# Encoder layer on one core: a sixth Strassen group in the input projection, and attention whose instructions stand in text order on every engine

## The chip, the cores and the metric

One core of a Trainium2 chip runs the whole layer. The metric is the device time of one execution in microseconds (us). The kernel before takes 1931.56 us, the median of 3 runs (1931.3 to 1931.82).

## The reference, cut to what matters

The input x is 1024 tokens by 1024 features in float32; the tokens form a grid of 16 by 64.

```python
h = x + 0.5 * swiglu(rms_norm(x, ffn1_norm), ...)          # D_FF = 2816
u = rms_norm(h, mix_norm)
z = u @ w_in                                               # 1024 x 4352
qa, ka, va, qb, kb, vb, ga, gb = split(z)
ya = neighbourhood_attention_2d(qa, ka, va, na_rpb)        # 8 heads of 64, bias by offset
yb = windowed_gqa_sink(rope(qb), rope(kb), vb, sink_logit) # 8 heads, 2 for k and v, window 128
merged = sigmoid(ga) * (ya @ w_branch_a) + sigmoid(gb) * (yb @ w_branch_b)
h = h + merged @ w_out
h = h + 0.5 * swiglu(rms_norm(h, ffn2_norm), ...)
return rms_norm(h, final_norm)
```

## The kernel before

**Arithmetic.** Every float32 factor is kept as a high part and a low part (`split`: ScalarE copies the high part, VectorE subtracts to get the low part, L93 and L94). A product is then three matmuls (`mm3`, L145, L147, L149: high times high, high times low, low times high). A matmul works on 128 x 128 weights and 512 columns.

**Stages.** The first FFN's hidden layer (an order written by hand), its down projection together with the norm that yields u, the input projection, attention, the two branch projections, the merge with w_out, the second FFN, the last norm. The FFNs, w_out and most columns of w_in go by Strassen: `products` takes two pairs of 128 columns as a group and makes 7 products of 24 matmuls with 512 columns for it, where plain multiplication takes 4 x 48 matmuls. VectorE makes the sums of blocks, and `store_z` brings the results out.

**The input projection.** w_in has 34 column blocks of 128. Five Strassen groups (`groups`) make 20 of them, the q, k and v blocks and two of the 16 gate blocks (numbers 18 to 33). The 14 gate blocks left (`gates`) are multiplied plainly, and serve as filler in attention.

**Attention.** 64 units go through a pipe three deep: 32 of the windowed GQA (`units_b`), then 32 of the neighbourhood attention (`units_a`). A unit is two heads' scores for 128 queries. Its three steps are

- `scores` (S): 4 matmuls into two banks of tag d (L1294, L1295); VectorE adds the bias and takes the minimum of the negated row (L1299), ScalarE takes exp with the row's sum (L1302), VectorE the reciprocal (L1305) and scales one head (L1306), ScalarE scales the other (L1307);
- `turn` (T): 6 transposes into two more banks of tag d (L1315), and a split of each (L93, L94);
- `values` (V): 6 matmuls into a bank of tag g (L1334, in units_a L1329), a copy on ScalarE (L1247, L1268) and additions on VectorE (`write`, L1249, L1269, L1272).

There are 4 banks of tag d and 4 of tag g. The loop over n issues S of unit n, filler, T of unit n-1, filler, V of unit n-2. The filler is a generator: `gate` yields after each of its 8 steps of 6 matmuls into two banks of tag g. At step 4 the next gate's weights are split (`load_w`, 128 x 1024), and at its end ScalarE copies the two banks out (L1143). `rate` lets 1.66 steps through per unit. After the last gate, `branch_b` (8 blocks of 4 steps) multiplies yb by w_branch_b: it splits a weight block (128 x 512), opens the gate with a sigmoid (L1195, 128 x 1024) and multiplies each bank by it (L1213). `branch_a` then does the like for ya. `units_a` adds bias and mask itself (`load_bias`, L1089).

**Who sets the order.** In the program of before a scheduler orders attention: the text hands it the instructions, and it places them on each engine's queue by its own estimate of what is ready. Only the first stage is ordered by hand. Each engine then takes its queue from the front and waits on semaphores.

## Time and profile before

| what | value |
| --- | --- |
| median of 3 runs | 1931.56 us |
| the profiled execution | 1931.21 us |
| its span, first to last instruction | 1929.4 us |
| mean granted TensorE clock | 0.999 |
| PE (matmul) busy | 1919.3 us, 99% |
| DVE (VectorE) busy | 1434.0 us, 74% |
| ACT (ScalarE) busy | 944.2 us, 49% |
| POOL (GpSimd) busy | 296.1 us, 15% |
| moved by DMA | 298.70 MB, 155 GB/s |

The profiled execution is 1.8 us longer than its span, and stands 0.35 us under the median. On the time axis of the trace, the groups of the input projection stand at about 675 to 843 us, attention at about 844 to 1126 us, the branch projections behind it. The views used below are the page (busy times, the chain that ended last, the groups of instructions), the waits of PE, the timeline of one engine (start, duration, engine, line, operation, output <- inputs, shape, and in brackets the idle time before and what ended it), and tables of busy time by stretch. A matmul's duration in the timeline overlaps the next one's: the distance between two starts says what a matmul costs.

### The profile page before, as it was taken

The page shows a single profiled execution, that of the slowest core. Times are in us where ns is not written, and L with a number is a line of the kernel's source. Part 1 is how long each engine was busy: PE and PEld are TensorE (multiplying, and loading weights), DVE is VectorE, ACT ScalarE, POOL GpSimd, SP SyncE. Part 2 cuts the span into 40 slices and gives each one's busy share as a digit, 9 for nine tenths or more (in the row PEclk, how much of TensorE's full clock was granted, in tenths as well). Part 3 has the DMA queues.
Part 4 walks back from the last instruction along what each step waited for, and adds up shares of the span by engine and source line. Part 5 has one row for each costly group of instructions (what it writes and reads, how often), then busy time and mean ns, then how long its engine had stood idle before and what let it go on. Part 6 is the DMA issues. An engine that isn't in the chain of part 4 may idle for free.

```text
span 1929.4 us, 25478 instructions
## 1 busy us (share of the span) xinstructions
PE 1919.3 (99%) x8956; PEld 1602.7 (83%) x8956; DVE 1434.0 (74%) x2560; ACT 944.2 (49%) x1826; POOL 296.1 (15%) x432
## 2 busy tenths in 40 slices
PE   9999999999999999999999999999999999999998
PEld 8888888888888888888888888888888888888886
DVE  8987765668957778678888856889676566569864
ACT  7532333344446543477777862365333333344453
POOL 0011100013300112211122231010111001005210
PEclk9999999999999999999999999999999999999999
DMA  6244323285334467753459676443422322493341
GB/s 267 95 167 166 138 100 125 87 298 215 92 106 138 158 202 240 218 166 102 116 130 195 188 240 212 170 153 121 147 98 103 127 87 106 145 340 114 115 142 61
DMA packets 151745, 298.70 MB, mean 155 GB/s; under 512 B 14912, under 2 KB 64448, under 8 KB 151616
## 3 DMA queue, kind: packets, MB, share of 16 engines
q1 hardware_dynamic: 123072, 210.53, 33.3%
q0 software_dynamic: 27824, 85.48, 13.3%
q8 instruction: 71, 1.16, 0.2%
q10 hardware_dynamic: 720, 1.05, 0.1%
q14 instruction: 58, 0.48, 0.1%
HBM read 210.50 MB, written 88.27 MB: 155 GB/s over the span
## 4 chain that ended last, share of the span: by engine, by line
PE 96%; DVE 2%; ACT 1%; DMA 0%; issue 0%; POOLq 0%; POOL 0%; DVEq 0%
PE g L145 18%; PE g L147 18%; PE g L149 18%; PE d L149 12%; PE d L145 12%; PE d L147 12%; PE d L1315 2%; PE g L1329 1%; PE d L1294 1%; PE d L1295 1%; PE g L1334 1%; PE d L138 1%; DVE ar L94 0%; DMA ahead<-in_w_in_dram 0%; DMA n1c<-in_ffn_norm_dram 0%
## 5 line engine op out<-in xcount | busy, mean ns | idle before, releaser
L145 PE MATMUL g<-ar,ws 128*128 128x512 f32 x1128 | 422.6, 395 | 0.3 <-DVE fa L602 0.3
L147 PE MATMUL g<-ar,ws 128*128 128x512 f32 x1128 | 416.7, 390 | 0.0
L149 PE MATMUL g<-ar,ws 128*128 128x512 f32 x1128 | 416.3, 390 | 0.0
L145 PE MATMUL d<-ar,ws 128*128 128x512 f32 x736 | 281.9, 390 | 0.5 <-ACT ws L309 0.5
L147 PE MATMUL d<-ar,ws 128*128 128x512 f32 x736 | 281.4, 389 | 0.1
L149 PE MATMUL d<-ar,ws 128*128 128x512 f32 x736 | 281.2, 389 | 0.1
L149 PEld LDWEIGHTS g<-ar,ws 128*128 128x128 f32 x1128 | 211.7, 188 | 44.8
L147 PEld LDWEIGHTS g<-ar,ws 128*128 128x128 f32 x1128 | 211.8, 188 | 44.6
L145 PEld LDWEIGHTS g<-ar,ws 128*128 128x128 f32 x1128 | 206.4, 188 | 36.4 <-issue 0.7
L312 DVE TENSOR_TENSOR ws<-raw,ws 128x512 fp32r<-128x512 f32 x204 | 139.3, 689 | 98.9 <-ACT ws L309 97.9
L309 ACT CAST ws<-raw 128x512 fp32r<-128x512 f32 x204 | 125.0, 620 | 142.2 <-PE g L149 63.8
L145 PEld LDWEIGHTS d<-ar,ws 128*128 128x128 f32 x736 | 138.1, 188 | 29.4 <-ACT ws L309 0.9
L147 PEld LDWEIGHTS d<-ar,ws 128*128 128x128 f32 x736 | 138.1, 188 | 29.3 <-DVE ar L814 0.5
L149 PEld LDWEIGHTS d<-ar,ws 128*128 128x128 f32 x736 | 138.1, 188 | 29.1 <-DVE ws L312 0.5
L93 ACT CAST ws<-raw 128x512 fp32r<-128x512 f32 (+1 forms) x121 | 81.0, 669 | 144.7 <-PE d L149 66.7
L94 DVE TENSOR_TENSOR ws<-raw,ws 128x512 fp32r<-128x512 f32 (+1 forms) x119 | 94.0, 792 | 60.7 <-ACT ws L93 60.5
L415 POOL DMA_DIRECT2D hid<-fx x91 | 49.3, 542 | 432.3 <-DVE fx L475 288.6
L93 ACT CAST ar<-raw 128x512 fp32r<-128x512 f32 (+1 forms) x83 | 56.0, 679 | 93.7 <-PE g L147 55.0
L94 DVE TENSOR_TENSOR ws<-ar,ws 128x512 fp32r<-128x512 f32 x114 | 98.2, 866 | 4.0 <-ACT ws L93 3.9
L145 PE MATMUL g<-ws,ws 128*128 128x512 f32 x232 | 90.9, 392 | 0.0
L149 PE MATMUL g<-ws,ws 128*128 128x512 f32 x232 | 90.4, 390 | 0.0
L147 PE MATMUL g<-ws,ws 128*128 128x512 f32 x232 | 90.3, 389 | 0.0
(313 smaller groups left out, 3604.8 us busy)
## 6 DMA issues: line engine op xcount, KB each, us to landing
raw<-hid SPq DMA_DIRECT2D x70, 512.0 KB
hid<-fx POOLq DMA_DIRECT2D x91, 256.0 KB, 2.3
ar<-in_ffn_w_down_dram SPq DMA_DIRECT2D x32, 512.0 KB
raw<-in_ffn_w_up_dram SPq DMA_DIRECT2D x31, 512.0 KB
raw<-in_ffn_w_gate_dram SPq DMA_DIRECT2D x27, 512.0 KB
raw<-in_w_in_dram SPq DMA_DIRECT2D x27, 512.0 KB
hid<-fa POOLq DMA_DIRECT2D x51, 256.0 KB, 2.6
ar<-zs_d POOLq DMA_DIRECT2D x48, 256.0 KB, 5.0
```

The source lines that it names most:

```text
L93: nc.scalar.copy(dst_hi, src)
L94: (eng or nc.vector).tensor_tensor(dst_lo, src, f32v(dst_hi), op=ALU.subtract)
L138: nc.tensor.transpose(pt[:, c * P:(c + 1) * P], xs[:, (half * 4 + c) * P:(half * 4 + c + 1) * P], ident)
L145: nc.tensor.matmul(b, lhs[0], r[0], start=first, stop=False, **kw)
L147: nc.tensor.matmul(b, lhs[0], r[1], start=False, stop=False, **kw)
L149: nc.tensor.matmul(b, lhs[1], r[0], start=False, stop=last, **kw)
L309: nc.scalar.copy(w[0][:, :512], a)
L312: nc.vector.tensor_tensor(w[0][:, 512:], a, f32v(w[0][:, :512]), op=ALU.subtract)
L415: nc.gpsimd.dma_start(hid[PRODUCTS.index(p), i], src)
L1294: nc.tensor.matmul(b[:, :nw], un["q"][s], un["kd"][s][:, k0 * P:k1 * P], start=True, stop=False)
L1295: nc.tensor.matmul(b[:, :nw], un["q"][s], un["kl"][s][:, k0 * P:k1 * P], start=False, stop=True)
L1315: nc.tensor.transpose(pt[:, i * P:(i + 1) * P], un["pr"][s][:, i * P:(i + 1) * P], ident)
```

## The change

1. **A sixth group.** The gate blocks 20 to 23 join the Strassen groups; 10 gates are left to attention.
2. **Text order.** `attention()` stands in a block that keeps the order of the text on VectorE, ScalarE, TensorE and the two queues that issue DMAs. The scaling of the probabilities (`scaled`) is taken out of `scores` and stands behind `turn`. `write` is cut in two: the copy stays in `values`, the addition follows the next unit's scores.
3. **Filler in halves.** A step of 6 matmuls now yields after 3. Each of the two filling calls of a unit gets 1.6 halves while n < 50, then 2, then 3 from n = 62, so that a gate (16 halves) takes exactly five units, and `branch_b` (64 halves) and the first part of `branch_a` (12) stand inside the attention.
4. **Gates by tanh.** sigmoid(x) becomes (tanh(x/2) + 1) / 2: a tanh on ScalarE, and (t + 1) times the bank in one VectorE instruction (L1293); the half goes into the scale of w_out's down projection (1.0 becomes 0.5). One ACT_TABLE_LOAD is gone from the program (4, now 3).
5. **Bias and mask.** The 16 additions of L1089 move to the first FFN's down projection and go by way of DRAM (`bm_d`); `fetch_bias` reads them back.
6. **Buffers and places.** The last group's results use another ring of slots; two early weight loads of the groups use other tiles and are issued at t = 0 and 1, not 3 and 4; u is fetched early; a unit's sink copies and its two output additions of 64x128 become one each; the splits of y (128 x 1024) move from GpSimd to VectorE.

```diff
+    def mm3_halves(banks, first, last, lhs, rhs):
+
+        parts = [(w, b, r[k], k) for w, k in ((0, 0), (0, 1), (1, 0)) for b, r in zip(banks, rhs)]
+        for i, (w, b, r, k) in enumerate(parts):
+            nc.tensor.matmul(b, lhs[w], r, start=first and w + k == 0, stop=last and w == 1)
+            if i == 2:
+                yield
...
+    bm_d = dram.tile([8, 2, P, 384], F32, name="bm_d")
...
+    def bias_add(h):
+        for e in range(2):
+            o = biased[0][4 + e]
+            pin(nc.vector.tensor_tensor(o.rearrange("p (d r w) -> p d r w", d=3, r=ROWS),
+                                        biased[0][2 + h % 2].rearrange("p (r d w) -> p d r w", d=3, w=8),
+                                        biased[0][e].rearrange("p (d r w) -> p d r w", d=3, r=ROWS), op=ALU.add))
...
-    groups = [[(12, 13), (14, 15)], [(16, 17), (0, 1)], [(4, 5), (8, 9)], [(2, 3), (6, 7)], [(10, 11), (18, 19)]]
+    groups = [[(12, 13), (14, 15)], [(16, 17), (0, 1)], [(4, 5), (8, 9)], [(2, 3), (6, 7)], [(10, 11), (18, 19)],
+              [(20, 21), (22, 23)]]
...
+    def gate_split(late=False):
+        h, l, r = ws4(), ws4(), mix["gate"]
+        split(h, l, r, None, late)
+        mix["gate"] = [a.rearrange("p (c f) -> p c f", f=P) for a in (h, l)]
...
+    held = [main.tile([P, 512], F32, tag="hs", bufs=6, name=nm_("hs")) for _ in range(6)]
+
+    def bias_at(hp, s, e):
+        k = 2 * (hp % 2) + s
+        return held[k][:, :384] if e else fa[:, 384 * k:384 * k + 384]
+
+    def fetch_bias(hp):
+        for s in range(2):
+            for e in range(2):
+                nc.sync.dma_start(bias_at(hp, s, e), bm_d[2 * hp + s, e])
...
         w = mix.pop("gate")
         bs = [bank("g"), bank("g")]
         for k, c in enumerate((4, 5, 6, 7, 0, 1, 2, 3)):
-            mm3(bs, k == 0, k == NC8 - 1, (w[0][:, c, :], w[1][:, c, :]), [u_half(c, n) for n in range(2)])
-            yield
+            yield from mm3_halves(bs, k == 0, k == NC8 - 1, (w[0][:, c, :], w[1][:, c, :]), [u_half(c, n) for n in range(2)])
+            if k < NC8 - 1:
+                yield
             if k in steps:
...
         gt = xs4()
         for n in range(2):
             nc.scalar.copy(gt[:, n * 512:(n + 1) * 512], bs[n])
         nc.gpsimd.dma_start(g_d[dc * P:(dc + 1) * P, :], gt)
+        yield
...
+    def open_gate(dc):
+        r = mix["rb", dc]
+        pin(nc.scalar.activation(r, r, AF.Tanh, scale=0.5))
+
+    def split_w(i):
+        mix["w", i] = branch_w(nc.gpsimd if i >= 10 else None, mix.pop(("wr", i)))
 
     def branch_b():
 
-        for c in range(2, 4):
-            split_y(Y_B[c], c * P, nc.vector if c == 2 else nc.gpsimd)
         for g in (4, 6):
             new_ar(g, F32)
-        nxt = branch_w(wb[0], 0, nc.vector), gate_b(0)
+        split_y(Y_B[2], 2 * P, nc.vector)
         for dc in range(NC8):
-            w, rb = nxt
             bs = [bank("dg"[dc % 2]) for _ in range(2)]
-            yield from branch_mm(bs, w, Y_B)
-            if dc + 1 < NC8:
-                nxt = branch_w(wb[0], dc + 1, nc.vector), gate_b(dc + 1)
+            mm = branch_mm(bs, mix.pop(("w", dc)), Y_B)
+            for c in range(4):
+                drain(mm, 1)
+                yield
+                drain(mm, 1)
+                if c < 3:
+                    yield
+                if c == 0:
+                    if dc == 0:
+                        split_y(Y_B[3], 3 * P, nc.vector)
+                    split_w(dc + 1)
+                    fetch_w(dc + 2)
+                elif c == 1:
+                    open_gate(dc)
+                    if dc + 1 < NC8:
+                        fetch_gate(dc + 1)
+            rb = mix.pop(("rb", dc))
...
             for n in range(2):
                 sl = slice(n * 512, (n + 1) * 512)
-                nc.vector.tensor_tensor(merged(dc)[:, sl], bs[n], rb[:, sl], op=ALU.mult)
+                nc.vector.scalar_tensor_tensor(out=merged(dc)[:, sl], in0=rb[:, sl], scalar=1.0, in1=bs[n],
+                                               op0=ALU.add, op1=ALU.mult)
+            yield
...
     def filler():
         for dc, nxt in zip(gates, gates[1:] + [None]):
             if nxt is not None:
-                yield from gate(dc, {4: lambda: mix.update(gate=load_w(win[0], GA + nxt * P))})
+                yield from gate(dc, {0: lambda: gate_fetch(nxt, raw4()), 5: gate_split})
             else:
-                yield from gate(dc, {0: lambda: [fetch_y(c * P) for c in range(2)],
-                                     4: lambda: [split_y(Y_B[c], c * P, nc.gpsimd) for c in range(2)],
-                                     5: lambda: [fetch_y(c * P) for c in range(2, 4)]})
+                yield from gate(dc, {0: lambda: [fetch_w(0), fetch_w(1)] + [fetch_y(c * P) for c in range(2)],
+                                     2: lambda: fetch_gate(0),
+                                     4: lambda: [split_y(Y_B[0], 0, nc.vector), fetch_y(2 * P)],
+                                     5: lambda: split_w(0),
+                                     6: lambda: [split_y(Y_B[1], P, nc.vector), fetch_y(3 * P)]})
         yield from branch_b()
         for i in range(2):
             branch_a(i)
-            for _ in range(3):
-                drain(a_mm[i][1], 1)
-                yield
+            for c in range(3):
+                for _ in range(2):
+                    drain(a_mm[i][1], 1)
+                    yield
...
                     lo = mix["lo"][:HD, c % 2]
                     nc.scalar.copy(lo, o[HD:])
-                    for s in range(2):
-                        nc.vector.tensor_tensor(ybox["b"][s * HD:s * HD + HD, c, :], o[:HD, s, :], lo[:, s, :], op=ALU.add)
+                    yield
+                    nc.vector.tensor_tensor(ybox["b"][:, c], o[:HD], lo, op=ALU.add)
...
+        un["sums"] = ssum, rc
+
+    def scaled(un):
+
+        ssum, rc = un["sums"]
         nc.vector.reciprocal(rc, ssum)
         nc.vector.tensor_scalar_mul(un["pr"][0], un["pr"][0], rc[:, 0:1])
         nc.scalar.activation(un["pr"][1], un["pr"][1], AF.Copy, scale=rc[:, 1:2])
...
+    n_b = 50
+    spent = 0.0
+
+    def filling(n):
         nonlocal spent
-        spent += rate * share
+        spent += len(gates) * 8 / n_b if n < n_b else 2 if n < 62 else 3
         drain(fill, int(spent))
...
+    def attention():
+
+        nonlocal pipe, prep
+        rest = iter(())
+        for n in range(1 << 30):
+            got = next(source, None)
+            if got is not None:
+                scores(got)
+            drain(rest)
+            pipe.insert(0, got)
+            for hp, n0 in preps.items():
+                if n == n0:
+                    prep = prep_a(hp)
+            if prep:
+                drain(prep, 1)
+            filling(n)
+            if len(pipe) > 1 and pipe[1] is not None:
+                turn(pipe[1])
+            if got is not None:
+                scaled(got)
+            if prep:
+                drain(prep, 1)
+            if n >= 26 and (n - 26) % 8 == 0 and n < 58:
+                fetch_bias((n - 26) // 8)
+            if n in (56, 57, 59):
+                fetch_y(512 + min(n - 56, 2) * P)
+            if n in (59, 60, 62):
+                split_y(Y_A[min(n - 59, 2)], 512 + min(n - 59, 2) * P, nc.vector)
+            filling(n)
+            if len(pipe) > 2 and pipe[2] is not None:
+                rest = values(pipe[2])
+            pipe = pipe[:3]
+            if not any(pipe):
+                break
+        drain(rest)
+        drain(fill)
+
+    by_text[0] = True
+    with tc.manual_schedule(engines={E.DVE, E.Activation, E.PE, E.SP, E.Pool}):
+        attention()
+    by_text[0] = False
...
-    down = Down(4, wo[0], 1.0, place, quarter, {k: left_d[i] for i, k in enumerate(("P5", "P6", "P3", "P7"))},
+    down = Down(4, wo[0], 0.5, place, quarter, {k: left_d[i] for i, k in enumerate(("P5", "P6", "P3", "P7"))},
```

Three places show what moved. First PE, at the change from one gate to the next among the units of GQA. The banks g_7085 and g_7086 belong to the gate that ends, g_7346 and g_7347 to the next; L162 is the filler's matmul, L1440 V, L1397 and L1398 S, L1421 T. In before, L145 to L149 are the filler, g_7514 and g_7515 the gate that ends, g_7758 and g_7759 the next, L1315 T. PE before:

```order
L147 MATMUL g_7514<-ar_4446,ws_7401 128x512
L147 MATMUL g_7515<-ar_589,ws_7401 128x512
L149 MATMUL g_7514<-ar_4446,ws_7402 128x512
L149 MATMUL g_7515<-ar_589,ws_7402 128x512
L1315 MATMUL d_7742<-ident,fa 128x128 x3
L1315 MATMUL d_7748<-ident,fa 128x128 x3
L145 MATMUL g_7758<-ar_4447,ws_7673 128x512
L145 MATMUL g_7759<-ar_4812,ws_7673 128x512
```

PE after:

```order
L1440 MATMUL g_7322<-ws_7242,fx_6195 128x256
L1440 MATMUL g_7322<-ws_7243,fx_6195 128x256
L1397 MATMUL d_7334<-ar_4873,ar_4874 128x384
L1398 MATMUL d_7334<-ar_4873,ar_4874 128x384
L1397 MATMUL d_7339<-ar_4873,ar_4874 128x384
L1398 MATMUL d_7339<-ar_4873,ar_4874 128x384
L162 MATMUL g_7346<-ar_4496,ws_7285 128x512
L162 MATMUL g_7347<-ar_4875,ws_7285 128x512
L162 MATMUL g_7346<-ar_4496,ws_7285 128x512
L1421 MATMUL d_7353<-ident,fa 128x128 x3
L1421 MATMUL d_7359<-ident,fa 128x128 x3
```

Before, T stood between a gate's last filler and the next gate's first. Now V and S stand there, and three filler matmuls of the new gate follow S, the second of them on g_7347.

Second, ScalarE at the same place. ws_7285 is the next gate's high part, g_7085 and g_7086 the banks that are copied out, ws_7295 the high parts of T's results, rc_7272 the reciprocals of this unit. ScalarE before, at the like place (L1302 exp, L93 split, L1307 scale, L1143 copy of a gate's bank):

```order
L1302 ACTIVATE fa,ssum_7656<-fa,nmx_7655 128x385 x2
L93 CAST ws_7685<-d_7687 128x3x128
L93 CAST ws_7685<-d_7693 128x3x128
L1307 ACTIVATE fa<-fa,rc_7657 128x384
L1247 COPY s_692_6541<-g_7705 64x256
L1302 ACTIVATE fa,ssum_7717<-fa,nmx_7716 128x385
L1143 COPY xs_7754<-g_7514 128x512
L1302 ACTIVATE fa,ssum_7717<-fa,nmx_7716 128x385
L93 CAST ws_7740<-d_7742 128x3x128
L1307 ACTIVATE fa<-fa,rc_7718 128x384
L93 CAST ws_7740<-d_7748 128x3x128
L1143 COPY xs_7754<-g_7515 128x512
```

ScalarE after (L1403 exp, L98 split, L1413 scale, L1205 copy of a gate's bank):

```order
L1403 ACTIVATE fa,ssum_7271<-fa,nmx_7270 128x385 x2
L98 CAST ws_7285<-raw_7110 128x1024
L98 CAST ws_7295<-d_7297 128x3x128
L98 CAST ws_7295<-d_7303 128x3x128
L1413 ACTIVATE fa<-fa,rc_7272 128x384
L1205 COPY xs_7318<-g_7085 128x512
L1205 COPY xs_7318<-g_7086 128x512
L1346 COPY s_723_6847<-g_7322 64x256
L1403 ACTIVATE fa,ssum_7331<-fa,nmx_7330 128x385 x2
L98 CAST ws_7351<-d_7353 128x3x128
```

Before, the weight split (ws_7673) stood in the unit ahead of these rows, one bank copy stood between the two exps of the next unit, and the other behind its split of T. Now the weight split stands ahead of the split of T, and both bank copies stand behind the scale, all in one unit.

Third, VectorE in the branch part inside attention (units of neighbourhood attention). L1293 opens the gate on the two banks of a branch block, L1400 is the score's bias and minimum, L1367 and L1370 the output additions, L101 the low part of a split, L1411 the reciprocal, L1412 the scale. VectorE after:

```order
L1367 TENSOR_TENSOR s_723_6847<-g_9607,s_723_6847 64x256
L1370 TENSOR_TENSOR fa<-g_9607,s_723_6847 64x128 x2
L101 TENSOR_TENSOR ws_9638<-d_9640,ws_9638 128x3x128
L101 TENSOR_TENSOR ws_9639<-d_9646,ws_9639 128x3x128
L1411 RECIPROCAL rc_9615<-ssum_9614 128x2
L1412 TENSOR_SCALAR fa<-fa,rc_9615 128x384
L1293 SCALAR_TENSOR_TENSOR ar_9562<-raw_9383,d_9566 128x512
L1293 SCALAR_TENSOR_TENSOR ar_9562<-raw_9383,d_9567 128x512
L1400 ISA fa,nmx_9671<-d_9674,fa 128x384
L1400 ISA nmx_9671 128x1
```

The two gate multiplications stand between one unit's scale and the next unit's scores; before, all of them came behind the attention, with no scores left.

More of the change, by code (lines that the diff above doesn't have):

```diff
@@ L90, in ws4, with pin, split @@
         return main.tile([P, 1024], F32R, tag="ws", bufs=8, name=nm_("ws"))
-    def split(dst_hi, dst_lo, src, eng=None):
-        nc.scalar.copy(dst_hi, src)
+    by_text = [False]
+    def pin(ins):
+        return ins if by_text[0] else tc.keep_in_program_order(ins)
+    def split(dst_hi, dst_lo, src, eng=None, late=False):
+        hi = nc.scalar.copy(dst_hi, src)
+        if late:
+            pin(hi)
         (eng or nc.vector).tensor_tensor(dst_lo, src, f32v(dst_hi), op=ALU.subtract)
@@ L1058, in trunk_kernel @@
     hook(2, gate_first)
+    hook(5, fetch_u)
     hook(1, keep_u)
-    pg = products(lambda i, m, half: w_cols(win[0], groups[i][m][half] * P), NG, store_z, at_end, (2, 3), range(8, 16),
-                  last=("P1", "P2", "P5", "P6", "P7", "P4", "P3"))
-    down.into(transition(down1, gain, to_strassen, behind(pg), 2), pg)
+    pg = products(lambda i, m, half: w_cols(win[0], groups[i][m][half] * P), NG, store_z, at_end, (2, 3),
+                  (*(NG - 1) * [*range(8, 16)], 12, 13, 10, 11, 8, 9, 14, 15),
+                  last=("P1", "P2", "P5", "P6", "P7", "P4", "P3"), early_rooms=(1, (2, 0)))
+    down.into(transition(down1, gain, to_strassen, behind(pg, (0, 1)), 2), pg)
     kept.clear()
@@ L1215, in filler, with a_open @@
+    def a_open(i):
+        r = mix["ra", i]
+        pin(nc.scalar.activation(r, r, AF.Tanh, scale=0.5))
     def filler():
@@ L1255, in units_b @@
                            kd=[kd_b()[g]] * 2, kl=[kl_b()[g]] * 2, v=[mix["vb"][g]], bias=[mask_b] * 2,
-                           sink=[nsk[:, 2 * c + s:2 * c + s + 1] for s in range(2)], write=write)
+                           sink=nsk[:, 2 * c:2 * c + 2], write=write)
     def units_a():
@@ L1279, in units_a @@
                 yield dict(j=j, q=[qs[s][:, tj] for s in range(2)], kd=kd, kl=kl, v=va,
-                           bias=[bias_slot(s)[:, edge, :] for s in range(2)], sink=None, write=write)
+                           bias=[bias_at(hp, s, edge) for s in range(2)], sink=None, write=write)
     npair = [0]
```

187 lines of the change are left out of this document (91 added, 96 removed).

## The prediction

> **What bounds the kernel now.** I read the page first, its busy times and its chain, then the waits of PE.
>
> ```profile
> PE 1919.3 (99%) x8956; PEld 1602.7 (83%) x8956; DVE 1434.0 (74%) x2560; ACT 944.2 (49%) x1826; POOL 296.1 (15%) x432
> PE 96%; DVE 2%; ACT 1%; DMA 0%; issue 0%; POOLq 0%; POOL 0%; DVEq 0%
> ```
>
> ```profile
> PE g L733 <- POOL ident masks.py:199: 1.5, 1, 1.5
> PE d L145 <- ACT ws L309: 0.5, 1, 0.5
> PE d L1315 <- DVE ws L94: 0.3, 1, 0.3
> PE g L145 <- DVE fa L602: 0.3, 1, 0.3
> ```
>
> PE is the bound from end to end: four waits, 2.6 us in all. So a matmul that goes is worth its full cost, a wait that appears is paid in full, and an edit elsewhere is worth nothing while PE doesn't wait. The mean of a 512-column matmul on the page (about 390 ns) is not its cost, since matmuls overlap. The timeline of PE shows it:
>
> ```profile
> 21.38 0.39 PE L145 MATMUL g<-ar,ws 128*128 128x512 f32 x1
> ...
> 31.61 0.39 PE L145 MATMUL g<-ar,ws 128*128 128x512 f32 x1
> ```
>
> 45 matmuls start between these two rows: 10.23 / 45 = 0.227 us each. Next, one unit of attention on PE:
>
> ```profile
> 908.25 0.34 PE L1294 MATMUL d<-ar,ar 128*128 128x384 f32 x1
> 908.43 0.34 PE L1295 MATMUL d<-ar,ar 128*128 128x384 f32 x1
> ...
> 908.95 0.63 PE L145 MATMUL g<-ar,ws 128*128 128x512 f32 x2
> ...
> 910.34 0.82 PE L1315 MATMUL d<-ident,fa 128*128 128x128 f32 x6
> 910.91 0.71 PE L145 MATMUL g<-ar,ws 128*128 128x512 f32 x2
> ...
> 912.39 0.88 PE L1334 MATMUL g<-ws,fx 128*128 128x256 f32 x6
> 913.11 0.34 PE L1294 MATMUL d<-ar,ar 128*128 128x384 f32 x1
> ```
>
> S takes 0.70 (908.25 to 908.95), six fillers 1.39, T 0.57, six more 1.48, V 0.72: 4.86 with four halves of filler, and 0.70 less, 4.16, with three. That is the pace the other engines must hold. How close they are, by stretches (PE, PEld, DVE, ACT, POOL busy, clock, DMA share, GB/s):
>
> ```profile
> 720.00:760.00 40.00, 40.00 (x178) 33.12 (x177) 33.14 (x46) 12.99 (x22) 9.84 (x17) 1.00 0.76 229
> 846.00:906.00 60.00, 60.00 (x353) 52.68 (x352) 49.25 (x175) 47.55 (x124) 8.29 (x14) 1.00 0.39 110
> 1026.00:1086.00 60.00, 60.00 (x362) 52.71 (x361) 54.12 (x171) 49.72 (x126) 13.10 (x19) 1.00 0.68 164
> ```
>
> In attention VectorE works 82 to 90% of the time and ScalarE 79 to 83%, and PE still doesn't wait, because the scheduler's order lets one unit's work run inside another's gaps. An order with less overlap has little room. These are the durations and distances it is made of, on ScalarE and on VectorE:
>
> ```profile
> 906.02 0.48 ACT L93 CAST ws<-d 128x384 fp32r<-128x384 f32 x1 [0.60 <-PE d L1315]
> 906.40 0.62 ACT L1302 ACTIVATE fa<-fa,nmx 128x385 f32<-128x385 f32 x1
> 906.92 0.19 ACT L1302 ACTIVATION_READ_ACCUMULATOR fa<-fa,nmx 128x1 f32 x1
> 907.01 0.47 ACT L93 CAST ws<-d 128x384 fp32r<-128x384 f32 x1
> 907.37 0.62 ACT L1307 ACTIVATE fa<-fa,rc 128x384 f32<-128x384 f32 x1
> 907.89 1.04 ACT L93 CAST ws<-raw 128x1024 fp32r<-128x1024 f32 x1
> ...
> 909.47 0.62 ACT L1302 ACTIVATE fa<-fa,nmx 128x385 f32<-128x385 f32 x1
> ```
>
> ```profile
> 906.54 0.56 DVE L94 TENSOR_TENSOR ws<-d,ws 128x384 fp32r<-128x384 f32 x1 [0.18 <-ACT ws L93]
> ...
> 907.23 0.14 DVE L1298 COPY fa<-nsk 128x1 f32<-128x1 f32 x1
> ...
> 908.81 0.62 DVE L1299 CUSTOM_DVE_ANT_0 fa<-d,masks,nsk 128x384 f32<-128x384 f32 x1 [0.58 <-PE d L1295]
> ...
> 910.52 1.22 DVE L94 TENSOR_TENSOR ws<-raw,ws 128x1024 fp32r<-128x1024 f32 x1
> 911.65 0.15 DVE L1305 RECIPROCAL rc<-ssum 128x2 f32<-128x2 f32 x1
> 911.88 0.56 DVE L94 TENSOR_TENSOR ws<-d,ws 128x384 fp32r<-128x384 f32 x1
> 912.35 0.41 DVE L1306 TENSOR_SCALAR fa<-fa,rc 128x384 f32<-128x384 f32 x1
> 912.68 0.55 DVE L94 TENSOR_TENSOR ws<-d,ws 128x384 fp32r<-128x384 f32 x1
> ```
>
> **What goes.** Four gates of 4 x 48 = 192 matmuls become 7 x 24 = 168. 24 x 0.227 = **-5.4 us**. The seventh share of VectorE's sums is hidden: in the groups' stretch above it works 33.1 of 40 us beside a full PE. PE's two waits at the transition (L309, L602: 0.8) may go with the earlier loads: between 0 and 0.8, I take **-0.7**, since both loads are issued three steps sooner. In attention the largest gap of PE is this one:
>
> ```profile
> 968.42 0.44 PE L1315 MATMUL d<-ident,fa 128*128 128x128 f32 x2 [0.34 <-DVE ws L94]
> ```
>
> Added up over 846 to 1128 us, the starts of like neighbours lie 1.9 further apart than they usually do. **-1.9** if the new order had no such gap; the waits' row alone would give 0.3. Moving the bias additions, 16 of about half a microsecond, frees VectorE in attention but no time of PE; in the down projection they lie beside a full PE, and cost 8.5 there if nothing covered them. The table load that goes was off PE's path: 0. Branch filler moved into attention costs PE the same matmuls: 0.
>
> **The loop of the new order.** In text order VectorE can't start unit n+1's bias (L1400) before it has scaled unit n (L1412). That closes a loop through two queues. From the rows: bias to exp 0.66 (908.81 to 909.47), exp to exp 0.61 and exp to split 0.61 (906.40 to 907.01), high part to low part 0.52 (906.02 to 906.54), low to low 0.47 and low to reciprocal 0.47 (911.88 to 912.35), reciprocal to scale 0.23, scale to the next 0.33 (912.35 to 912.68): 3.90, and with the sink's copy (0.14) about 4.05 in GQA. PE's step is 4.16 or 4.86. The plain units just fit, without room; whatever text order adds to the loop shows.
>
> **The gate's change.** It comes nine times, in a unit with four halves. Time from S: bias at 0.56 (908.25 to 908.81), exps 1.22 and 1.83, then the next gate's high part 2.44. It lasts 1.04, and as every instruction there starts about 0.1 before the end of the last, T's high part follows at 3.38. The gate's low part starts at 3.55 and holds VectorE 1.13 (910.52 to 911.65), T's low parts 4.68 and 5.15, reciprocal 5.62, ScalarE's scale 5.85. Only behind that come the two bank copies:
>
> ```profile
> L1143 ACT COPY xs<-g 128x512 f32<-128x512 f32 x28 | 16.2, 592 | 2.2 <-PE d L1315 1.6 <-PE g L149 0.2
> ```
>
> The first starts at 6.37 (0.52 behind the scale, as 907.37 to 907.89) and ends at 6.96. The new gate's second matmul takes that bank, and PE stands ready for it at 4.86 + 0.70 + 0.23 = 5.79: it waits 1.2. Behind it stand the rest of the filler, T, V and the next S. 9 x 1.2 = **+10.8**. It would be nothing if the copy came before the scale.
>
> The Trainium skill (Perfetto Trace Analysis, section Tensor Engine Instruction) says that ScalarE and VectorE are strict FIFO. If a ready copy could overtake the waiting scale, it would run some 2 us earlier and this term would be 0. None of the rows above has a ready instruction behind a waiting one, so this trace neither bears the rule out nor speaks against it.
>
> **The branch part, n = 48 to 62.** Two units make a block. Costs of its own, none shown between scores before; the nearest rows:
>
> ```profile
> L1195 ACT ACTIVATE xs<-xs 128x1024 f32<-128x1024 f32 x8 | 8.5, 1061 | 10.8 <-DMA xs<-g_d 9.0 <-DVE ar L1213 1.8
> L93 ACT CAST ws<-raw 128x512 fp32r<-128x512 f32 x20 | 12.4, 620 | 20.3 <-PE g L149 8.1 <-issue 5.0 <-DMA raw<-in_w_branch_b_dram 3.7
> L94 DVE TENSOR_TENSOR ws<-raw,ws 128x512 fp32r<-128x512 f32 x18 | 12.8, 726 | 6.6 <-ACT ws L93 6.5
> L602 DVE SCALAR_TENSOR_TENSOR fa<-g,fa 128x512 f32<-128x512 f32 x8 | 5.2, 680 | 0.0
> ```
>
> In a block's first unit the weight's high part stands behind ScalarE's scale, so its low part starts 0.23 + 0.52 + 0.62 + 0.05 = 1.42 behind the reciprocal and takes 0.6, where the next bias otherwise came 0.56 behind it: +1.5, a loop of 5.4. In the second the tanh (as the sigmoid, 0.95 from start to start) stands ahead of T's split, and the two gate multiplications (as L602, 0.6 each) ahead of the next bias: 3.9 + 0.95 + 1.2 = 6.0. The mean of 5.7 against PE's 4.86 is 0.84; twelve units: +10. Seven splits of y, now VectorE's, lengthen their units like the gate's split (6.18 - 0.56 = 5.6, not 4.05): 7 x 1.5 = 10.5, and the last heads' preparation 2; the units with slack take back 2, and the units at the end, six halves long or without scores, 3.5. **+17** in all; between 0, if the pipe's depth hid it, and 30, if nothing were taken back. I take 17 since its terms are all on one loop.
>
> Preparations earlier, start and end: **+2**. Sum: -5.4 - 0.7 - 1.9 + 10.8 + 17 + 2 = +21.8, on the profiled execution's 1931.2 (span 1929.4 and 1.8 around it; 0.4 under the median): **1953**.
>
> **The rivals.** *All hidden*: the queues run ahead enough, and only what goes counts: 1931.2 - 8.0 = 1923. For it speaks that plain units fit (4.05 under 4.16) and that the pipe is three deep; against it that the bank copy is late by the queue, not by load. It decides at the copy's end: under 5.79 from S, and block loops under 4.86. *Only the gates' changes*: the branch part is covered by the depth, 1923 + 10.8 + 2 = 1936. *The clock*: PE has to stay busy for its clock. The table by stretches at the end of the trace:
>
> ```profile
> 1925.00:1929.00 4.00, 0.00 (x0) 0.00 (x0) 0.47 (x1) 0.43 (x1) 0.00 (x0) 0.57 0.35 131
> ```
>
> Without a matmul the granted clock falls to 0.57 within 4 us. If each of some 21 waits cost a stretch like it at half rate, 2 us of PE's work each, half of it inside waits anyway, that adds 20: 1973. My waits are 0.8 to 1.5 long, so I give it little. The Trainium skill (TensorE: Matmul & The Clock Gate, Part 1) has the clock halve after an idle window of about 3.4 us; by that rule waits of this length change nothing, in agreement with the forecast. *No saving*: the sixth group gives back its 5.4 in waits on VectorE's sums: 1958, inside my range.
>
> **How the numbers follow.** Forecast 1953 (1940 to 1963) 0.60; only the gates 0.18; all hidden 0.15; clock or worse 0.07. Within 0.2% (3.9 us, about what a measurement here can tell from no change) is 1927.7 to 1935.4. Faster is the hidden case, 0.15; same is the edge between it and the gates, 0.07; slower 0.78. The range leaves out the hidden case and half of the worst: 1930 to 1966.
>
> **What would show it.** Right: PE's waits list L162 <- ACT on L1205 nine times at about 1.2, and in the branch part T or S <- ACT or DVE by 0.5 to 1.5 per unit; the page's slices of the groups stay full, and 24 fewer matmuls. The clock stays 1.00. Wrong: PE full through attention (hidden), waits at gates alone, or waits on DMAs (bm_d, w_branch_b), which I cost at nothing since the DMA share in attention is 0.39 to 0.68.

## The result, and the profile after

The changed kernel takes 1974.9 us (median of 5 runs, 1972.99 to 1976.55) against 1931.56: a ratio of 1.0223, 95% interval 1.0208 to 1.0238. It is 43.3 us slower; 21.8 was forecast. From the page, the busy times and the chain:

```profile
PE 1930.6 (98%) x8932; PEld 1601.8 (81%) x8932; DVE 1449.8 (73%) x2529; ACT 949.1 (48%) x1836; POOL 286.2 (15%) x428
PE 69%; issue 18%; DVE 5%; ACT 3%; POOL 3%; DMA 1%; POOLq 0%; SPq 0%; ACTq 0%; DVEq 0%
```

The 24 matmuls are gone (8956, now 8932), and the chain leaves PE for a third of the span. PE's waits, where there were four rows before:

```profile
PE g L162 <- ACT xs L1205: 12.9, 8, 2.2
PE d L1421 <- DVE nmx L1400: 7.3, 8, 2.1
PE d L152 <- DVE raw L1557: 2.2, 1, 2.2
PE d L162 <- DVE ws L101: 2.1, 3, 1.0
PE g L162 <- DVE nmx L1400: 2.1, 1, 2.1
PE d L1421 <- DVE ar L1293: 1.6, 1, 1.6
```

The first and the fifth are the nine changes of gate. The second (but for 0.3), fourth and sixth are the branch part. The third is new and was not forecast: it lies in the merge behind attention. Two stretches of the table (PE, PEld, DVE, ACT, POOL busy, clock, DMA share, GB/s), one in the groups and one in attention:

```profile
720.00:760.00 40.00, 40.00 (x178) 33.14 (x177) 33.10 (x47) 12.95 (x23) 9.82 (x17) 1.00 0.75 224
...
940.00:980.00 40.00, 36.31 (x206) 31.64 (x205) 27.20 (x85) 29.13 (x71) 2.57 (x4) 0.96 0.29 86
```

The groups are full as before. In attention PE waits 3.7 of 40 us, VectorE and ScalarE are *less* busy than before (27 and 29 of 40, or 68 and 73%), and the granted clock falls under 1. No engine is full there: what is late is late by its place in a queue.

**A change of gate, seen closely.** The first one, on PE, on ScalarE and on VectorE:

```profile
895.99 0.40 PE L162 MATMUL g<-ar,ws 128*128 128x512 f32 x1
898.53 1.14 PE L162 MATMUL g<-ar,ws 128*128 128x512 f32 x2 [2.15 <-ACT xs L1205]
```

```profile
893.06 0.62 ACT L1403 ACTIVATE fa<-fa,nmx 128x385 f32<-128x385 f32 x1 [0.27 <-DVE nmx L1400]
...
894.27 1.03 ACT L98 CAST ws<-raw 128x1024 fp32r<-128x1024 f32 x1
895.33 0.65 ACT L98 CAST ws<-d 128x256 fp32r<-128x256 f32 x2
897.39 0.61 ACT L1413 ACTIVATE fa<-fa,rc 128x384 f32<-128x384 f32 x1 [1.42 <-DVE rc L1411]
897.92 1.05 ACT L1205 COPY xs<-g 128x512 f32<-128x512 f32 x2
```

```profile
892.39 0.62 DVE L1400 CUSTOM_DVE_ANT_0 fa<-d,masks,nsk 128x384 f32<-128x384 f32 x1
...
895.34 1.23 DVE L101 TENSOR_TENSOR ws<-raw,ws 128x1024 fp32r<-128x1024 f32 x1 [1.45 <-ACT ws L98]
896.48 0.75 DVE L101 TENSOR_TENSOR ws<-d,ws 128x256 fp32r<-128x256 f32 x2
897.14 0.16 DVE L1411 RECIPROCAL rc<-ssum 128x2 f32<-128x2 f32 x1
```

ScalarE stands idle 1.42 in front of the scale while the finished gate waits behind it to be copied: the mechanism of the prediction, row for row. From bias to copied bank it takes 6.1, where 6.4 was worked out (T's parts are narrower in this unit). But PE waits 2.3 between the two starts (2.54 less the usual 0.23), not 1.2, because the bias itself starts 1.5 behind its unit's S and not 0.56. At this first change that lag is left over from the start of attention (2.26 at unit 0, 1.51 here). Why the later changes find a lag, the plain units show (VectorE, two units in a row):

```profile
911.69 0.42 DVE L1412 TENSOR_SCALAR fa<-fa,rc 128x384 f32<-128x384 f32 x1
912.03 0.16 DVE L1394 COPY fa<-nsk 128x2 f32<-128x2 f32 x1
912.34 0.62 DVE L1400 CUSTOM_DVE_ANT_0 fa<-d,masks,nsk 128x384 f32<-128x384 f32 x1
...
914.85 1.02 DVE L101 TENSOR_TENSOR ws<-d,ws 128x384 fp32r<-128x384 f32 x2 [1.01 <-ACT ws L98]
915.78 0.15 DVE L1411 RECIPROCAL rc<-ssum 128x2 f32<-128x2 f32 x1
...
916.62 0.62 DVE L1400 CUSTOM_DVE_ANT_0 fa<-d,masks,nsk 128x384 f32<-128x384 f32 x1
```

From bias to bias 4.28, not 4.05, and PE's step is 4.16: each plain unit falls 0.12 further behind, and a gate's unit and the next (5.86 and 4.91 from bias to bias) much further. Over the later changes, too, the wait is 1.2 plus what the bias was late beyond 0.56: 1.56 with a lag of 0.93, 2.0 with 1.38.

**The clock.** Behind the wait at 896 it falls to half, behind the one at 944 it doesn't (the clock stands behind POOL's busy time):

```profile
895.24:898.65 3.41, 1.26 (x8) 0.88 (x8) 3.13 (x9) 1.97 (x6) 0.00 (x0) 1.00 0.21 58
898.65:902.06 3.41, 3.41 (x12) 2.82 (x13) 1.86 (x6) 2.77 (x8) 0.54 (x1) 0.50 0.70 252
...
943.03:946.44 3.41, 1.77 (x12) 1.39 (x10) 3.09 (x7) 1.92 (x5) 0.14 (x1) 1.00 0.61 127
946.44:949.85 3.41, 3.22 (x20) 2.83 (x21) 1.85 (x7) 3.07 (x9) 0.57 (x1) 1.00 1.10 369
```

PE works again from 898.5, and for 3.4 us at half rate: 1.7 us of its work lost. This comes five times in attention (at 898, 970, 1021, 1124 and 1178), 8.5 in all; before, not once. The five runs' times go with their mean clock, from 1972.99 us at 0.997 to 1976.55 at 0.994.

### The profile page after: what moved, and what is told of

The parts are those of the page before. It is cut to its first block, busy times and chain, and to the rows that moved or that the text cites. A ratio compares the mean times of both kernels' runs of the same rounds, so it can differ in the third digit from the quotient of the medians.

```text
span 1973.3 us, 25598 instructions
## 1 busy us (share of the span) xinstructions
PE 1930.6 (98%) x8932; PEld 1601.8 (81%) x8932; DVE 1449.8 (73%) x2529; ACT 949.1 (48%) x1836; POOL 286.2 (15%) x428
## 4 chain that ended last, share of the span: by engine, by line
PE 69%; issue 18%; DVE 5%; ACT 3%; POOL 3%; DMA 1%; POOLq 0%; SPq 0%; ACTq 0%; DVEq 0%
PE g L152 13%; PE g L154 13%; PE g L156 13%; PE d L156 10%; PE d L152 10%; PE d L154 10%; DVE ws L101 2%; ACT fa L1403 1%; POOL zs_d L950 1%; DMA ar<-zs_d 1%; PE g L162 1%; DVE ar L101 1%; ACT ws L98 1%; PE d L145 1%; POOL z_d L955 0%
## 5 line engine op out<-in xcount | busy, mean ns | idle before, releaser
L152 PE MATMUL g<-ar,ws 128*128 128x512 f32 x872 | 339.8, 390 | 0.0
L156 PE MATMUL g<-ar,ws 128*128 128x512 f32 x872 | 339.3, 389 | 0.0
L154 PE MATMUL g<-ar,ws 128*128 128x512 f32 x872 | 339.3, 389 | 0.0
L152 PE MATMUL d<-ar,ws 128*128 128x512 f32 x696 | 271.8, 391 | 0.4 <-ACT ws L330 0.2
L154 PE MATMUL d<-ar,ws 128*128 128x512 f32 x696 | 271.1, 389 | 0.6 <-DVE ar L865 0.6
L156 PE MATMUL d<-ar,ws 128*128 128x512 f32 x696 | 270.9, 389 | 0.3 <-DVE ws L333 0.2
L333 DVE TENSOR_TENSOR ws<-raw,ws 128x512 fp32r<-128x512 f32 x210 | 143.6, 689 | 107.2 <-ACT ws L330 106.2
L162 PE MATMUL g<-ar,ws 128*128 128x512 f32 x672 | 186.6, 410 | 15.0 <-ACT xs L1205 12.9
L152 PEld LDWEIGHTS g<-ar,ws 128*128 128x128 f32 x872 | 163.7, 188 | 34.2 <-DVE fa L983 0.3
L156 PEld LDWEIGHTS g<-ar,ws 128*128 128x128 f32 x872 | 163.7, 188 | 34.0
L154 PEld LDWEIGHTS g<-ar,ws 128*128 128x128 f32 x872 | 163.7, 188 | 33.8
L152 PEld LDWEIGHTS d<-ar,ws 128*128 128x128 f32 x696 | 130.6, 188 | 28.3 <-ACT ws L330 0.7
L154 PEld LDWEIGHTS d<-ar,ws 128*128 128x128 f32 x696 | 130.7, 188 | 28.1 <-DVE ar L865 1.2
L156 PEld LDWEIGHTS d<-ar,ws 128*128 128x128 f32 x696 | 130.6, 188 | 28.0 <-DVE ws L333 1.0
L162 PEld LDWEIGHTS g<-ar,ws 128*128 128x128 f32 x672 | 122.4, 193 | 37.5 <-ACT xs L1205 18.2
L98 ACT CAST ws<-raw 128x512 fp32r<-128x512 f32 (+1 forms) x107 | 70.3, 657 | 132.1 <-PE d L156 63.0
L101 DVE TENSOR_TENSOR ws<-raw,ws 128x512 fp32r<-128x512 f32 (+1 forms) x107 | 84.0, 785 | 59.8 <-ACT ws L98 59.7
L101 DVE TENSOR_TENSOR ws<-ar,ws 128x512 fp32r<-128x512 f32 x114 | 93.8, 828 | 11.4 <-ACT ws L98 11.4
L98 ACT CAST ar<-raw 128x512 fp32r<-128x512 f32 (+1 forms) x81 | 54.0, 669 | 88.9 <-PE g L154 54.4
L101 DVE TENSOR_TENSOR ws<-d,ws 128x384 fp32r<-128x384 f32 (+1 forms) x128 | 61.1, 519 | 41.9 <-ACT ws L98 41.8
```

What stands on the lines that cost most here:

```text
L98: hi = nc.scalar.copy(dst_hi, src)
L101: (eng or nc.vector).tensor_tensor(dst_lo, src, f32v(dst_hi), op=ALU.subtract)
L152: nc.tensor.matmul(b, lhs[0], r[0], start=first, stop=False, **kw)
L154: nc.tensor.matmul(b, lhs[0], r[1], start=False, stop=False, **kw)
L156: nc.tensor.matmul(b, lhs[1], r[0], start=False, stop=last, **kw)
L162: nc.tensor.matmul(b, lhs[w], r, start=first and w + k == 0, stop=last and w == 1)
```

## The experiments

All times are medians beside runs of the kernel before on the same chip (1931.6 to 1932.4); differences between versions are not corrected for the chip. To see where a change of time lies, I take the start of the first S matmul of units 0, 23, 50 and 63 from each timeline; the work on PE between them is the same, except that later branch blocks and the scheduler shift some filler past these marks. A half-clock stretch counts where it falls: in the change two lie up to unit 23, one behind it up to 50, two up to 63.

| kernel | us | units 0 to 23 | 23 to 50 | 50 to 63 |
| --- | --- | --- | --- | --- |
| the change | 1974.9 | 105.9 | 127.0 | 85.1 |
| scheduler in attention | 1931.2 | 93.5 | 113.1 | 68.0 |
| late scaling | 1957.4 | 100.6 | 120.9 | 78.6 |
| early sink copy | 1969.1 | 100.1 | 127.3 | 86.0 |
| both | 1951.1 | 95.7 | 118.2 | 78.8 |
| late scaling, branch blocks one call later | 1950.0 | 100.9 | 120.8 | 70.7 |
| text order with all that helped | 1941.5 | 95.6 | 118.2 | 70.7 |
| text order for n < 50 only | 1959.2 | 104.5 | 127.4 | 68.9 |

**1. Attention handed back to the scheduler**, all other parts of the change kept.

```diff
-    by_text[0] = True
-    with tc.manual_schedule(engines={E.DVE, E.Activation, E.PE, E.SP, E.Pool}):
-        attention()
-    by_text[0] = False
+    attention()
```

> The changed kernel with all its parts, but attention handed back to the scheduler instead of text order. Theory (the text order's loop through VectorE's and ScalarE's queues paces attention): most of the loss goes, 1924 to 1936 us. Rival (the loss comes from the branch projections inside attention, their splits on VectorE and the other buffers, whatever the order): it stays above 1950.

1931.2 us, ratio 0.9994 (0.9985 to 1.0003). The text order costs all 43 us, and nothing else in the change costs on balance. Against this kernel the change loses 26.2 up to unit 50 and 17.2 from there to unit 63.

**2. The sixth group alone**, in the kernel before.

```diff
-    groups = [[(12, 13), (14, 15)], [(16, 17), (0, 1)], [(4, 5), (8, 9)], [(2, 3), (6, 7)], [(10, 11), (18, 19)]]
+    groups = [[(12, 13), (14, 15)], [(16, 17), (0, 1)], [(4, 5), (8, 9)], [(2, 3), (6, 7)], [(10, 11), (18, 19)],
+              [(20, 21), (22, 23)]]
...
-    pg = products(lambda i, m, half: w_cols(win[0], groups[i][m][half] * P), NG, store_z, at_end, (2, 3), range(8, 16),
+    pg = products(lambda i, m, half: w_cols(win[0], groups[i][m][half] * P), NG, store_z, at_end, (2, 3),
+                  (*(NG - 1) * [*range(8, 16)], 12, 13, 10, 11, 8, 9, 14, 15),
```

> The kernel before with the sixth Strassen group (and its ring of slots) alone. Theory: 24 matmuls fewer at 0.227 us each, 5.4 us less, 1926 (1924 to 1929), since VectorE's sums lie beside a full PE. Rival (the group gives its saving back in waits on VectorE, or attention runs short of filler): 1931 or more.

1939.2, ratio 1.0044 (1.0031 to 1.0056): the rival is right. PE's waits in that kernel, from an execution of 1944.1, 4.9 over the median, so that they may be larger than usual:

```profile
PE d L1317 <- DVE fa L1308: 3.4, 2, 2.6
PE g L145 <- DVE fa L932: 2.3, 1, 2.3
...
PE d L1296 <- DVE ws L94: 1.2, 1, 1.2
```

Attention has four gates less to fill with, and T and S wait in it (L1317, L1296). The wait of 2.3 in the groups comes from VectorE's queue: there a step of the rotation stands ahead of the instruction that frees a bank (L932), and itself waits for its DMA:

```profile
744.62 1.22 DVE L965 TENSOR_TENSOR xs<-xs,fx 128x1024 f32<-128x1024 f32 x1 [4.07 <-DMA xs<-z_d]
745.76 0.68 DVE L932 SCALAR_TENSOR_TENSOR fa<-d,hs 128x512 f32<-128x512 f32 x1
```

So the group alone doesn't pay. In the changed kernel the branch products fill in for the four gates, and with the scheduler its attention has none of these waits; which of its parts spares them wasn't tried one by one.

**3. Late scaling.** `scaled(got)` behind the second filling, so that the bank copies stand ahead of the scale.

```diff
-            if got is not None:
-                scaled(got)
...
             filling(n)
+            if got is not None:
+                scaled(got)
```

> The changed kernel with the unit's scaling moved behind the second filling, so that a gate's two bank copies stand ahead of the scale on ScalarE. If the copy's place is what costs (the prediction's term, each wait by itself): the waits on the copy go, 13 to 17 us less than the changed kernel, 1958 to 1962. If the loop as a whole paces the units (5.85 in a gate's unit, 4.91 in the next, 4.28 in plain ones against PE's 4.86 and 4.16): only the 0.6 of the next unit goes per gate, 4 to 6 us less plus a few us of half clock, 1965 to 1971, and PE waits elsewhere.

1957.4, 17.5 less: the copy's place costs, as the first theory had it. PE's waits there:

```profile
PE d L1421 <- DVE fa L1394: 4.2, 7, 0.7
PE d L1421 <- DVE nmx L1400: 3.3, 4, 1.1
PE d L1421 <- DVE fa L1412: 3.2, 4, 1.2
...
PE g L162 <- ACT xs L1205: 1.1, 5, 0.3
```

The copy's 12.9 became 1.1. 5.3 of the gain lies up to unit 23, 6.1 from 23 to 50, and 6.5 in the branch part, where the weight splits and the gate multiplications also come to stand ahead of the scale. Of these, 3.4, 1.7 and 3.4 are half-clock stretches, of which attention has none left. One has come behind the merge's wait, so that 6.8 less is lost that way in all. Some waits came back in another place, T waiting on VectorE (first row), which is the loop.

**4. Early sink copy.** The copy for the next unit's sink is made ahead of T's low parts.

```diff
-        if ext:
+        if ext and npair[0] < 2:
             nc.vector.tensor_copy(both[:, :, 0], un["sink"])
...
+        if un["sink"] is not None and npair[0] < 32:
+            c = npair[0] % 4
+            nxt = fa[:, 1536 + 2 * (npair[0] % 2) * 385:][:, :770].rearrange("p (s k) -> p s k", s=2)
+            nc.vector.tensor_copy(nxt[:, :, 0], nsk[:, 2 * c:2 * c + 2])
```

> The changed kernel with the copy of the sink for the next GQA unit made ahead of T's low parts, where VectorE is idle, instead of between scale and bias. If the loop paces the units: plain units fall from 4.28 to about 4.0, under PE's 4.16, five units from 23.6 to 22.1, six periods, 9 us less, with fewer half-clock stretches 9 to 13 less: 1962 to 1966. If only the copy's place costs: 0 to 2 less, 1973 to 1975.

1969.1, 5.8 less, short of the 9 to 13 and more than the 2 of the rival. Up to unit 23 it is 5.8 less, but 3.4 of that are the two half-clock stretches that are gone. Behind, nothing shows: units of neighbourhood attention have no sink, and what units 23 to 31 gain is hidden by one stretch more than in the change (at 1013 and 1061, where the change has one at 1021). Plain units now take 3.97 to 4.16, the bias starts 0.55 behind S again, and a change of gate then costs what the prediction said:

```profile
987.21 0.40 PE L162 MATMUL g<-ar,ws 128*128 128x512 f32 x1
988.68 0.50 PE L162 MATMUL g<-ar,ws 128*128 128x512 f32 x1 [1.07 <-ACT xs L1205]
```

1.47 between starts, 1.24 over the usual; four of the first five changes come to 1.24 or 1.25, the other five to 1.3 to 2.1. So the loop's length and the copy's place both count: the first sets how late the second begins.

**5. Both.**

> The kernel with the scaling behind the second filling (1957.4) and the early sink copy together. There the gate's wait is gone and T waits on the sink's copy instead (4.2 in all). If the plain loop of 4.28 is what is left in GQA: it falls to 4.0, those waits go, 4 to 6 less, 1951 to 1954. If the gain of the early copy alone (5.8) came only through the gate's wait: 0 to 2 less, 1955 to 1957.

1951.1, 6.3 less than late scaling alone, all of it up to unit 50 (4.9 and 2.7 in the profiled runs). Neither of the two has a half-clock stretch in attention, so this is what the copy's place is worth by itself. The waits of T on the sink's copy are gone. GQA is then 2.2 behind the scheduler over 23 units.

**6. The splits of y on GpSimd**, with late scaling (`nc.vector` becomes `nc.gpsimd` in the five calls).

> The kernel with the late scaling (1957.4) and the seven splits of y on GpSimd as before. By the prediction's term for them (7 x 1.5 on VectorE's part of the loop): 8 to 11 less, 1946 to 1950. If the branch part's loss is not in VectorE's queue (ScalarE's part of these splits, weights, banks): 0 to 3 less, 1954 to 1957.

1963.7, 6.3 *more*. That row of the prediction can't be confirmed this way: GpSimd takes twice as long for a split, and in text order the split stands in its queue behind DMA issues that wait for the last heads' preparation.

```profile
1101.28 0.51 POOL L1168 DMA_DIRECT2D ar<-zs_d  x1 [1.28 <-DMA ar<-zs_d]
1103.15 0.51 POOL L1168 DMA_DIRECT2D ar<-zs_d  x1 [1.36 <-DMA ar<-zs_d]
...
1105.38 0.51 POOL L1170 DMA_DIRECT2D ar<-zs_d  x1 [0.60 <-DMA ar<-zs_d]
1105.91 2.35 POOL L101 TENSOR_TENSOR ar<-raw,ar 128x1024 fp32r<-128x1024 f32 x1
```

PE waits 5.8 for that one split (L162 <- POOL). What the seven splits cost on VectorE stays open.

**7. Branch blocks one call later**, with late scaling: the first filling call of unit 50 gives nothing.

```diff
+        if n == n_b and first:
+            return
```

> The kernel with the late scaling (1957.4) and every branch block begun one filling call later (n = 50's first call gives nothing), so that the two gate multiplications stand in the gap in which VectorE waits for T's split, and the tanh ahead of the scale. If the place in the queue is what costs in the branch part: about 1 to 2 less per block of two units, six blocks, 6 to 12 less, 1945 to 1951. If it is the work itself (VectorE and ScalarE too full with a branch block in a unit): 0 to 3 less, and 1 to 2 more for the empty call, 1955 to 1959.

1950.0, 7.4 less, all of it from unit 50 to 63 (78.6 to 70.7), though one half-clock stretch came (at 1103). The same work in other places. In the change the two gate multiplications hold the next bias up. With late scaling alone they stand ahead of the reciprocal (multiplications at 1113.45, reciprocal at 1114.64), and still hold it up by 1.2; here they stand in the gap ahead of T's low parts. The tanh, too, leaves its place ahead of T's split for the gap before the scale. VectorE in the change, then with later blocks:

```profile
1141.37 0.42 DVE L1412 TENSOR_SCALAR fa<-fa,rc 128x384 f32<-128x384 f32 x1
1141.70 1.28 DVE L1293 SCALAR_TENSOR_TENSOR ar<-xs,g 128x512 f32<-128x512 f32 x2
1142.90 0.55 DVE L1400 CUSTOM_DVE_ANT_0 fa<-d,fa 128x384 f32<-128x384 f32 x1
```

```profile
1113.65 0.42 DVE L1412 TENSOR_SCALAR fa<-fa,rc 128x384 f32<-128x384 f32 x1
1113.99 0.55 DVE L1400 CUSTOM_DVE_ANT_0 fa<-d,fa 128x384 f32<-128x384 f32 x1
...
1116.00 1.28 DVE L1293 SCALAR_TENSOR_TENSOR ar<-raw,d 128x512 f32<-128x512 f32 x2
1117.20 1.02 DVE L101 TENSOR_TENSOR ws<-d,ws 128x384 fp32r<-128x384 f32 x2
```

From scale to bias 1.53 in the first, 0.34 in the second.

**8. The merge's sums partly on GpSimd**, with the scheduler in attention.

```diff
-            nc.vector.tensor_tensor(s[i], a, b, op=op)
+            (nc.gpsimd if i == 3 else nc.vector).tensor_tensor(s[i], a, b, op=op)
...
-        nc.vector.tensor_tensor(merged(dc), merged(dc), r, op=ALU.add)
+        (nc.gpsimd if i in (4, 6) else nc.vector).tensor_tensor(merged(dc), merged(dc), r, op=ALU.add)
```

> The changed kernel with attention by the scheduler (1931.2) and four of the combining sums and two of the merge's additions on GpSimd. If PE's wait of 2.3 in the merge comes from VectorE, which lost the time of branch_b's products beside which it worked: the wait goes, 2 to 3 less, 1928 to 1930, and below the kernel before by its interval. If not: 1930 to 1932.

1929.2, ratio 0.9986 (0.9977 to 0.9994): the one version that is faster than the kernel before by its interval, if by little. The merge's wait, first without, then with GpSimd's help:

```profile
PE d L152 <- DVE raw L1554: 2.3, 1, 2.3
```

```profile
PE d L152 <- DVE raw L1554: 1.6, 1, 1.6
```

VectorE is full there, 20.00 of 20 us from 1190 to 1210 without help and 19.88 with it. The wait shrank by 0.6 only (2.25 to 1.63); another 1.7, a half-clock stretch behind it, went as well. So the time came out as expected mostly by the clock, and the runs of the two versions overlap (1928.15 to 1932.09 without, 1927.81 to 1931.04 with help). In text order (experiment 9) the same help takes the wait from 2.3 to 0.5.

**9. Text order with all that helped**: late scaling, early sink copy, later branch blocks, the merge's sums.

> Text order with all that helped it: late scaling, early sink copy, branch blocks one call later, and the merge's sums partly on GpSimd. If the pieces add (17.5, 6.3, 7.4 and 2.0 off 1974.9): 1940 to 1944. If the places share one wait: 1945 to 1950. In either case still above the kernel before.

1941.5, ratio 1.0047 (1.0030 to 1.0064). The pieces add. Text order is still 10 behind the scheduler (12 behind it with the merge's sums moved as well, 1929.2), 5.1 of it from unit 23 to 50, where the preparations of the heads fall.

**10. Text order for n < 50 only**, the scheduler behind it.

```diff
     with tc.manual_schedule(engines={E.DVE, E.Activation, E.PE, E.SP, E.Pool}):
-        attention()
+        attention(0, 50)
     by_text[0] = False
+    attention(50, 1 << 30)
```

> The changed kernel with text order only for n < 50, and the scheduler for the rest (the branch part). Read from the starts of S in the traces of text order and scheduler (0 apart at n = 0, 26.2 at n = 50, 43.4 at n = 63): 17 less, 1956 to 1960. If the branch part's loss were the consequence of a pipe that comes late into it, and not of its own order: 1965 or more.

1959.2, 15.7 less: the branch part's loss is its own, and the front's is 28.

**11. PE kept busy in the gate's wait.** Each gate but the first repeats its first matmul five times ahead of itself, in the free bank; each repeat is overwritten by the next.

```diff
+        if dc != gates[0]:
+            for _ in range(5):
+                nc.tensor.matmul(bs[0], w[0][:, 4, :], u_half(4, 0)[0], start=True, stop=True)
```

> The changed kernel with the first matmul of each gate but the first issued five more times ahead of itself (into the bank that is already free; each repeat is overwritten, 5 x 0.23 = 1.1 us), so that PE works in most of the wait for the bank copy. If the half clock behind three of these waits comes from PE's idleness: those stretches go, 3 to 6 less, 1969 to 1972. If the clock falls for another reason: 1973 to 1976. If the waits are not there to be filled: nine times 1.1 more, 1983 or above.

1972.1, 2.8 less with 45 matmuls more, at the edge of what was expected if idleness is the cause; the clock decides. The clock over the front:

```profile
880.00:900.00 20.00, 18.34 (x104) 15.40 (x103) 13.71 (x51) 14.22 (x42) 0.54 (x1) 1.00 0.34 104
900.00:940.00 40.00, 39.04 (x229) 34.37 (x228) 28.06 (x89) 29.61 (x74) 2.02 (x3) 1.00 0.18 53
940.00:980.00 40.00, 38.65 (x226) 33.60 (x225) 28.04 (x87) 30.16 (x74) 2.73 (x5) 1.00 0.29 86
980.00:1020.00 40.00, 37.22 (x220) 31.95 (x219) 27.56 (x86) 28.83 (x74) 8.71 (x16) 1.00 0.71 165
1020.00:1060.00 40.00, 39.42 (x232) 34.22 (x231) 29.38 (x97) 30.01 (x82) 8.79 (x16) 1.00 0.64 162
```

No half clock in the front any more, where the change has three stretches. It came from PE's idleness in those waits. But three stretches of 1.7 are 5.1, and 2.8 came back. The 45 repeats cost 10.2 of PE's time and fill 9.3 of the 15.0 it was idle at the changes, so these are no shorter; from unit 0 to 50 it is 3.5 less (232.9 to 229.4). Elsewhere the profile has three stretches where the change has two.

## Why the prediction was wrong

The direction was right, and so were the mechanisms of the gate's change and of the branch part; the size was half. Forecast +21.8, measured +43.3; the 21.5 between them are, by its steps, 8.0 that were not saved, 5.8 more at the gate's changes, 8.5 of half clock that had no term, 2.5 more at preparations, start and end, and 3.2 less in the branch part.

- **What goes, -8.0: not kept.** The matmuls went. But with the scheduler in attention the whole change comes out at 1931.2, level with before. The merge's wait (2.3), a half-clock stretch behind it (1.7) and two waits of 0.8 and 0.9 in the branch part took the saving of 5.4 back. "Branch filler moved into attention costs PE the same matmuls: 0" forgot what the branch products had covered: with them gone, VectorE's sums in the merge have less PE work beside them. The rival *no saving* came near on this step, by another way than it named: the groups stayed full.
- **The plain units "just fit, without room": this step failed.** The loop was given 4.05 and measured 4.28, over PE's 4.16. Two distances were off: from exp to split 0.72 (909.33 to 910.05), not 0.61, and from the sink's copy to the bias 0.31 in place of 0.15. That is enough to turn a slack of 0.11 into a lag of 0.12 per unit, and the lag is paid at the next change of gate. Experiment 4 takes it away and finds 1.24 at a change without the lag.
- **The gate's change, +10.8: mis-sized by that lag**, and at the first change by the lag that attention starts with. Nine waits, by the distances of the starts 1.3 to 2.3 each, 16.6 in all (15.0 idle by the rows). The mechanism (copy behind scale) is shown by experiment 3.
- **The clock: a rival that came true in part.** It was given little since waits of 0.8 to 1.5 were forecast, and "The clock stays 1.00" stood among the signs of being right. Behind waits of 1.7 to 2.3 it fell five times, 8.5 in all; three times in the front, 5.1. Experiment 11 shows the cause there. (The 0.57 read in the prediction's last row was a mean: the clock was full until 1925.54, then half.)
- **The branch part, +17: measured 17.2** beside the scheduler from unit 50 to 63, and 15.7 by experiment 10. That it agrees so closely is luck: 3.4 of the 17.2 are two half-clock stretches, which the term did not hold, and 13.8 is the rest. Of its terms, the places of the gate multiplications, the tanh and the weight splits are shown together (7.9 by experiment 7; 6.5, of which 3.4 clock, by experiment 3). The seven splits of y are not: the attempt ran into another queue.
- **Preparations, start and end, +2.** The front's 26.2 less 16.6 and 5.1 leaves 4.5 for them and for what isn't split further. Two waits of S in the front, 0.9 and 0.6, end at the preparations' splits (`fx`, L101). In the best text order 5.1 stays between units 23 and 50; I didn't take the preparations out, so that they are its cause is argued, not shown.

*All hidden* and *only the gates* both fell. The rule that the queues are strict FIFO (the Trainium skill, Perfetto Trace Analysis, section Tensor Engine Instruction), which the prediction left undecided by its own trace, is borne out here: the finished gate's copy stood behind a scale that idled 1.42, and 12.9 of PE's waits fell to 1.1 when the two changed places.

## What to carry to other kernels

When an order is fixed by hand, write down the loop that closes through each in-order queue and compare its period, not the engine's busy share, with the bound engine's step. A loop some 3% over the step costs nothing at once and everything at the next long item, so keep it a margin under. Put what frees a resource ahead of instructions that wait, and long items of the filler where their engine idles anyway; and ask of work that is moved what it used to cover where it stood.

## What the runs showed of the hardware

The granted clock halved for about 3.4 us behind some of PE's waits, and behind others as long (at 944, 1065, 1113 and 1252 in the change) it didn't, so that the wait's length alone doesn't decide. Its place does. In all 13 traces the clock is either 1.00 or 0.50, and within a trace the slow stretches start on a grid of 3.413 us: in the change the five lie 21, 15, 30 and 16 steps apart. A step follows slow when PE was idle for about half of the one before it. Over all traces, start and end left out, each of the 22 steps with 1.8 us of idle PE or more is followed by a slow one, three of the six with 1.69 to 1.77 are, and none with 1.64 or less. The wait at 896 lies within one step, 2.15 us; the one at 944 crosses a border and leaves 1.64 in one and 0.19 in the next. So whether a wait of about 2 us costs another 1.7 is in part chance from one execution to the next.

The Trainium skill (TensorE: Matmul & The Clock Gate, Part 1) speaks of an idle window of about 3.4 us, free-running. The length of the slow stretch and the grid agree; that half a window suffices does not follow from a full idle window, and here the measurement decides.
